# Spacers in three SBUF pools: the stationary and the moving operand of most 512-column products begin at the same place of 512 bytes

## Chip, cores and metric

The kernel runs on one core of a Trainium2 chip. The metric is the device time of one execution in microseconds, the median of the runs of a kernel. Three runs of the kernel before lie within 0.8 us of each other (1016.72 to 1017.52), so 0.2% (2.0 us) is about what a measurement of it can tell from no change.

## What is computed

One layer of an encoder block on 1024 tokens of width 1024, in float32:

```
h = rmsnorm(x) * (1 + sc1) + sh1;  u_f, q, k, v = split(h @ w_in)
y_f = per-group 2-D Fourier mix of u_f and a 64x64 map
y_a = windowed attention: softmax(q k^T / 8 + bias, sink) v, blocks of 128 queries against 384 keys
x   = x + g1 * (concat(y_f, y_a) @ w_out)
h2  = rmsnorm(x) * (1 + sc2) + sh2
16 experts, each picks its 128 best tokens:  y = (silu(xin @ w_gate) * (xin @ w_up)) @ w_down
x   = x + g2 * scatter_add(gate * y)
```

Each of the 48 expert matrices is 1024x1024 float32, 4 MB. They are read once each.

## The kernel before

**Products in three terms.** A float32 operand is split into a high part, which the matmul takes as fp32r, and a low part, the remainder. `mm3` (lines 73 to 76) multiplies a pair of split operands with three matmuls: high by high (line 74), low by high (line 75), high by low (line 76). The first argument after the output is the *stationary* operand (128 columns of activations, 512 bytes in each partition), the second the *moving* one (512 columns of weights, 2048 bytes in each partition). Each matmul loads its own stationary operand while the matmul ahead of it streams its moving one.

**Experts.** The weights come in units of 1 MB (256 rows of a matrix). `load` (line 1037) brings a unit into one of 13 `raw` buffers in three pools; `cut_unit` (line 1056) splits it: ScalarE writes `wh` (line 79), VectorE `wl` (line 80). The tile pair comes from the pool `wa` or from the pool `wk`, two buffers of each in either:

```
wp = wa if place[m] % 4 in (0, 1) else wk
h = wp.tile([128, 2, D], F32R, name="wh", bufs=2)
```

The first 6 units of all are used without a split (`PLAIN`, line 1214). `product` uses up one unit: 2 blocks of 128 rows, 2 halves of 512 columns, 3 matmuls each, 12 matmuls. A product of an expert is 4 units, 48 matmuls; an expert has three products (gate, up, down). By the line above the first two units of each product lie in `wk` and the last two in `wa`. The stationary operands of the experts, `t0h`, `t0l`, `t1h` and `t1l`, all lie in `wk`; experts take `t0` and `t1` in turns, and the down products take the one that is free. So each product is 24 matmuls with both operands in `wk`, then 24 with the stationary operand in `wk` and the moving one in `wa`. Split units: 186, of which 94 lie in `wa` and 92 in `wk`. TensorE, VectorE, ScalarE, GpSimd and the queue on SyncE each run their instructions in the order written.

**Attention and out-projection.** `front` (lines 677 and 678) makes the logits of a head: stationary `qk` from the pool `pb`, moving `khi` and `klo`, 384 or 256 columns. The out-projection `oproj` uses `mm3` with the stationary operands `yh`, `yl`, `yah`, `yal` (pool `p3`, which is on the right side of SBUF) and the moving `woh`, `wol` (pools `po0` and `po`, placed behind `pb`): 8 tiles of 128 tokens, 48 matmuls each. Its steps are put between those of the attention by a fixed rate.

**Input projection.** `terms` (line 367) multiplies, for one stationary tile `hh` or `hl`, three moving pieces of 512, 512 and 256 columns. Weights of blocks 0 to 3 lie in the pool `pw`, those of blocks 4 to 7 in `p1`, where `hh` and `hl` lie as well. The change doesn't touch it.

**Where the tiles begin.** Pools are filled from their start, tile by tile, so a tile's address in each partition follows from what stands before it. Its remainder by 512 bytes, as the built program has it (all steps inside these tiles are whole multiples of 512 bytes, but for the key blocks and head pieces, which don't matter here):

```
product               stationary   before   after    moving        before   after
experts, from wk      t0*, t1*       96      288     wh, wl (wk)      96      288
experts, from wa      t0*, t1*       96      288     wh, wl (wa)     288      288
out-projection        yh, yah ...     0        0     woh, wol        192        0
logits                qk             64      480     khi, klo        480      480
input projection 0-3  hh, hl        256      256     wh, wl          256      256
input projection 4-7  hh, hl        256      256     wh, wl           64       64
```

Of the kernel before, what the change touches and what calls it, by code (L numbers as in the profile page):

```python
# [11 lines left out]
F32 = mybir.dt.float32  # L12
# [33 lines left out]
def block_kernel(ctx: ExitStack, tc: tile.TileContext, t_in, out):  # L46
# [9 lines left out]
    def pool(name, bufs=1, space=None, **kw):  # L56
        if space is None:
            return tc.tile_pool(name=name, bufs=bufs, reuse_waits="tile", **kw)
        return tc.tile_pool(name=name, bufs=bufs, space=space, **kw)

    cst = ctx.enter_context(pool("cst"))
    dram = ctx.enter_context(pool("dram", space=bass.MemoryType.DRAM))
    ps = ctx.enter_context(pool("ps", bufs=2, space=bass.MemoryType.PSUM))
    raw1 = ctx.enter_context(pool("raw1", bufs=RAW1))

    def pt(name="pt"):
        return ps.tile([128, 512], F32, name=name, tag="pt", bufs=2)

    def banks(stack, name, **tags):
        p = stack.enter_context(pool(name, space=bass.MemoryType.PSUM))  # L70
        return [lambda t=t, n=n: p.tile([128, 512], F32, name=t, tag=t, bufs=n) for t, n in tags.items()]
# [62 lines left out]
    def drain(g):  # L134
        for _ in g:
            pass
# [202 lines left out]
    p = pt()  # L339
# [20 lines left out]
    def terms(ts, kc, hs_, o):  # L360
        for l, r in ((0, w_h), (1, w_h), (0, w_l)):
            for s_ in range(len(ts)):
                lhs = hs_[l][:, o + s_ * 128:o + s_ * 128 + 128]
                for acc, c0, c1 in zip(accs[s_], (0, 512, 1024), (512, 1024, 1280)):

                    first = kc == 0 and l == 0 and r is w_h and not (s_ and c0 == 1024)
                    PE.matmul(acc[:, :c1 - c0], lhs, r[kc][:, c0:c1], start=first, stop=(kc == 7 and r is w_l),  # L367
                              skip_group_check=c0 == 1024)
            yield
# [60 lines left out]
    p = terms(pair, 0, hs.pop(0), 0)  # L430
# [62 lines left out]
    for m, (t, kc0) in enumerate(seq):  # L493
# [20 lines left out]
        for a in range(4):  # L514
            project((t,), kc0 + a, hs_, a * 128)
            if m == 0 and a == 1:
                DVE.scalar_tensor_tensor(gg, qg, HD ** -0.5, kg, op0=OP.mult, op1=OP.mult)
                p = pt()
# [21 lines left out]
    pb = p_b.enter_context(pool("pb"))  # L540
# [6 lines left out]


    pj, lgb, ypb = banks(p_b, "psB", pj=2, lg=3, yp=1)

    st = {}

# [96 lines left out]
    def qprep(t, kv):  # L649
        pq = pt()  # L650
        for hp in range(2):
            PE.transpose(pq[:, hp * 128:hp * 128 + 128], qn[t][:, (kv * 2 + hp) * 128:(kv * 2 + hp + 1) * 128], ident)
        qk = pb.tile([128, 2, 2, 128], F32R, name="qk", bufs=2)
        pqv = pq[:, :256].rearrange("p (a b) -> p a b", b=128)
        for par in range(2):
            hi_r = slice(par * 64, par * 64 + 64)
            lo_r = slice(64 - par * 64, 128 - par * 64)
            ACT.activation(qk[hi_r, :, par, :], pqv[hi_r], AF.Copy)
            DVE.tensor_tensor(qk[lo_r, :, par, :], pqv[hi_r], qk[hi_r, :, par, :].bitcast(F32), op=OP.subtract)
        qks[t, kv] = qk  # L660

    def front(t, kv):
        blocks = span(t)
        k0 = blocks[0] * 128
        wid = len(blocks) * 128
        j0 = k0 - (t - 1) * 128
        qk = qks.pop((t, kv))
        m = pb.tile([128, 4], F32, name="m", bufs=4)
        negm = pb.tile([128, 4], F32, name="negm", bufs=4)
        den = pb.tile([128, 4], F32, name="den", bufs=4)  # L670
        es = pb.tile([128, 4], F32, name="es", bufs=4)
        rin = pb.tile([128, 4], F32, name="rin", bufs=4)
        sk = sink[:, kv * 4:kv * 4 + 4]
        sbs = []
        for i in range(4):
            lg = lgb()
            PE.matmul(lg[:, :wid], qk[:, i // 2, i % 2, :], khi[:, kv, k0:k0 + wid], start=True, stop=False)  # L677
            PE.matmul(lg[:, :wid], qk[:, i // 2, i % 2, :], klo[:, kv, k0:k0 + wid], start=False, stop=True)  # L678
            sb = pb.tile([128, 384], F32, name="sb", bufs=SB)
            DVE.tensor_tensor_reduce(sb[:, :wid], lg[:, :wid], bias[:, kv * 4 + i, j0:j0 + wid], 1.0,  # L680
                                     sk[:, i:i + 1], op0=OP.add, op1=OP.max, accum_out=m[:, i:i + 1])
            sbs.append(sb)
            tick()
        yield
        DVE.tensor_scalar(negm, m, -1.0, None, op0=OP.mult)
        DVE.tensor_tensor(es, sk, m, op=OP.subtract)
        ACT.activation(es, es, AF.Exp)
        for i in range(4):
            ACT.activation(sbs[i][:, :wid], sbs[i][:, :wid], AF.Exp, bias=negm[:, i:i + 1],
                           accum_out=den[:, i:i + 1])  # L690
        yield
        DVE.tensor_tensor(den, den, es, op=OP.add)
        DVE.reciprocal(rin, den)
        for i in range(4):
            DVE.tensor_scalar(sbs[i][:, :wid], sbs[i][:, :wid], rin[:, i:i + 1], None, op0=OP.mult)
        fr[t, kv] = sbs
# [43 lines left out]
    def load_x2(t):  # L740
        xh = raw([128, 2, D])
        SP.dma_start(xh[:, 0], x[t * 128:(t + 1) * 128, :])
        yt = at0.tile([128, 4, 128], F32, name="yt", tag="qn0")
        SP.dma_start(yt, ydf[t])
        yh = p3.tile([128, 4, 128], F32R, name="yh", bufs=2)
        yl = p3.tile([128, 4, 128], F32R, name="yl", bufs=2)
        split(yh, yl, yt)
        xts[t] = xh, yh, yl
# [178 lines left out]
    def wo_cut():  # L927
        k, j = divmod(next(wo_next), 2)
        split(wo_h[k][:, j], wo_l[k][:, j], wo_raw[k][:, j])
# [6 lines left out]
    def filler2():  # L936
        rate[0] = RATE2
        for t in range(NT):
            for i, _ in enumerate(oproj(t)):
                if t == 0 and i == 1:  # L940
                    g2_prep()
                if t == 0 and i == 5:
                    router_prep()
                for _ in range(2 if t > 4 else 1):
                    next(srt, None)
                yield
# [3 lines left out]
    def tick():  # L950
        debt[0] += rate[0]
        while debt[0] >= 1.0:
            debt[0] -= 1.0
            next(fill[0], None)
# [3 lines left out]
    srt = sorter()  # L958
    po, p3 = None, None
    po0 = p_c.enter_context(pool("po0"))  # L960
    wo_h, wo_l = ([po0.tile([128, 2, D], F32R, name=f"wo{x}{k}") for k in range(3)] for x in "hl")
    wo_next = itertools.count()
    wo_v = w_out.rearrange("(k p) c -> p k c", p=128)
# [13 lines left out]
    for n in range(len(units) + 2):  # L977
        if n == NSW:
            for _ in fill[0]:
                for g in lateq:  # L980
                    next(g, None)
            for g in lateq:
                drain(g)
            p_f.close()
            p_u.close()
            po = p_c.enter_context(pool("po"))
            p3 = p_c.enter_context(pool("p3", side="right"))
            sp[0] = p3
            g1_r, sh2_r, G2_r = (p3.tile([128, D], F32, name=n_) for n_ in ("g1_r", "sh2_r", "G2_r"))
            wr, wrG = (p3.tile([128, 8, NE], F32, name=n_) for n_ in ("wr", "wrG"))  # L990
            cb = p3.tile([128, NE], F32, name="cb")
            load_x2(0)
            for i, r in enumerate((g1_r, sh2_r, G2_r)):
                SP.dma_start(r, md[i:i + 1, :].to_broadcast([128, D]))
            wo_h.append(po.tile([128, 2, D], F32R, name="woh3"))
            wo_l.append(po.tile([128, 2, D], F32R, name="wol3"))
            wo_cut()
            wo_cut()
            fill = [filler2()]
            SP.dma_start(wr, t_in["w_router"][0].rearrange("(k p) e -> p k e", p=128))  # L1000
        fg = front(*units[n]) if n < len(units) else iter(())
        bg = back(*units[n - 2]) if n >= 2 else iter(())
        next(fg, None)
        next(bg, None)
        next(fg, None)
        next(bg, None)
        next(bg, None)
        drain(fg)
        for g in lateq:
            for _ in range(9):  # L1010
                next(g, None)
        if n + 1 < len(units):
            qprep(*units[n + 1])
            tick()
        drain(bg)
# [10 lines left out]
    wk = ctx.enter_context(pool("wk"))  # L1026
# [41 lines left out]
        load()  # L1068

    pa, = banks(ctx, "psM", pa=6)  # L1070
    for m in EARLY:
        load(m)
    g2_r = wk.tile([128, D], F32, name="g2_r")
# [218 lines left out]
    for b in range(2):  # L1292
        p = pt()
# [120 lines left out]
```

## Time and profile before

| what | value |
|---|---|
| median of three runs | 1017.39 us |
| the profiled execution's own time | 1017.5 us |
| its span, first to last instruction | 1015.4 us |
| TensorE busy | 958.8 us, 94% of the span |
| VectorE, ScalarE, GpSimd busy | 787.4, 628.0, 403.8 us |
| stages | the input projection's first product starts at 19.36 us, the last of the out-projection stage is over by 411.07, the first expert product starts at 428.11 |

The span is shorter than the time by 2.1 us, which lie around it. The busy time of a matmul in the profile has a modelled end and overlaps the next one; how fast matmuls follow one another is read from their starts, or from how many stand in a stretch in which TensorE never waits.

### The profile page before, as it was taken

How to read it: one execution, taken by the hardware profiler on the slowest of the kernel's cores; microseconds unless marked ns; L12 is line 12 of the kernel's file. 1: busy time of each engine (PE TensorE's matmuls, PEld its weight loads, DVE VectorE, ACT ScalarE, POOL GpSimd, SP SyncE). 2: the span in 40 equal slices, each digit the busy share in tenths (PEclk: the TensorE clock that was granted, in tenths of full speed). 3: DMA queues.
4: the chain of work that ended last, by engine and by line, in shares of the span. 5: the costliest groups of instructions: out<-in, count | busy, mean ns of one | idle time of the engine just before them, and what ended most of it. 6: DMA issues, size and time to landing. Idle time of an engine off the chain costs nothing.

```text
span 1015.4 us, 13138 instructions
## 1 busy us (share of the span) xinstructions
PE 958.8 (94%) x4737; PEld 747.6 (74%) x4737; DVE 787.4 (78%) x1240; ACT 628.0 (62%) x832; POOL 403.8 (40%) x236
## 2 busy tenths in 40 slices
PE   4997999979999999599899999999999999999996
PEld 3676877756777777458788888888888888888884
DVE  1346865777666869779869888988988898899894
ACT  2473444666455553226667777777777777777772
POOL 0026453100000000000357669768776876782203
PEclk9998999989999999599999999999999999999998
DMA  9966664361222138889989999999999999999912
GB/s 292 337 231 248 253 266 126 97 201 53 87 80 73 54 139 304 319 324 352 374 309 385 378 376 411 381 379 399 390 377 379 411 377 380 390 397 379 380 60 41
DMA packets 91641, 283.95 MB, mean 280 GB/s; under 512 B 8140, under 2 KB 25728, under 8 KB 91448
## 3 DMA queue, kind: packets, MB, share of 16 engines
q1 hardware_dynamic: 86712, 266.32, 69.3%
q0 software_dynamic: 4864, 16.80, 6.5%
q8 instruction: 37, 0.61, 0.2%
q14 instruction: 28, 0.23, 0.1%
HBM read 263.79 MB, written 21.40 MB: 281 GB/s over the span
## 4 chain that ended last, share of the span: by engine, by line
PE 83%; DVE 6%; POOL 3%; issue 2%; ACT 2%; DMA 1%; SPq 1%; POOLq 0%; ACTq 0%; DVEq 0%
PE pa L74 17%; PE pa L75 17%; PE pa L76 16%; PE pu L367 5%; PE pt L1258 3%; PE yp L719 3%; PE pj L75 2%; PE pj L74 2%; PE pa L1217 2%; PE pj L76 2%; PE pt L706 2%; PE pt L829 2%; PE lg L677 1%; DVE ws L116 1%; PE lg L678 1%
## 5 line engine op out<-in xcount | busy, mean ns | idle before, releaser
L80 DVE TENSOR_TENSOR wl<-raw,wh 128x2048 fp32r<-128x2048 f32 (+1 forms) x189 | 423.3, 2267 | 64.4 <-ACT wh L79 62.9
L79 ACT ACTIVATE wh<-raw 128x2048 fp32r<-128x2048 f32 (+1 forms) x189 | 355.7, 1895 | 79.0 <-PE pa L75 73.9
L1231 POOL TENSOR_SCALAR oneh<-tri_f,pos 128x128 bf16<-128x128 f32 x96 | 210.3, 2206 | 15.2 <-PE pt L1239 14.9
L74 PE MATMUL pa<-wh,t1h 128*128 128x512 f32 x384 | 152.5, 397 | 0.0
L76 PE MATMUL pa<-wl,t1h 128*128 128x512 f32 x384 | 150.7, 392 | 0.0
L75 PE MATMUL pa<-wh,t1l 128*128 128x512 f32 x384 | 150.6, 392 | 0.0
L74 PE MATMUL pa<-wh,t0h 128*128 128x512 f32 x360 | 144.8, 402 | 0.0
L75 PE MATMUL pa<-wh,t0l 128*128 128x512 f32 x360 | 142.3, 395 | 0.0
L76 PE MATMUL pa<-wl,t0h 128*128 128x512 f32 x360 | 142.2, 395 | 0.0
L792 POOL TENSOR_TENSOR rs<-ss,mhalf 128x1 f32<-128x1 f32 x8 | 4.4, 555 | 221.0 <-DVE ss L790 194.0
L1273 POOL TENSOR_TENSOR ys<-ys,g_r 128x512 f32<-128x512 f32 x30 | 53.5, 1800 | 91.6 <-ACT ys L1272 91.6
L76 PEld LDWEIGHTS pa<-wl,t1h 128*128 128x128 f32 x384 | 72.0, 188 | 16.5
L75 PEld LDWEIGHTS pa<-wh,t1l 128*128 128x128 f32 x384 | 72.1, 188 | 15.6
L74 PEld LDWEIGHTS pa<-wh,t1h 128*128 128x128 f32 x384 | 72.0, 188 | 15.6
L76 PEld LDWEIGHTS pa<-wl,t0h 128*128 128x128 f32 x360 | 68.2, 190 | 15.8
L75 PEld LDWEIGHTS pa<-wh,t0l 128*128 128x128 f32 x360 | 68.3, 190 | 14.9 <-issue 0.2
L74 PEld LDWEIGHTS pa<-wh,t0h 128*128 128x128 f32 x360 | 68.2, 189 | 14.9 <-issue 0.2
L1248 POOL DMA_INDIRECT xe<-h2d,idx x16 | 18.7, 1170 | 150.9 <-DVE gt L1245 150.8
L1276 POOL DMA_INDIRECT out_dram<-ys,idx x16 | 51.1, 3196 | 11.0 <-DVE ys L1275 6.6
L680 DVE CUSTOM_DVE_ANT_0 sb<-lg,bias,sink 128x384 f32<-128x384 f32 (+1 forms) x64 | 35.3, 579 | 16.9 <-PE pt L706 10.6
L367 PE MATMUL pu<-wh,hh 128*128 128x512 f32 x128 | 43.6, 422 | 2.3 <-ACT hh L79 2.1
L708 ACT ACTIVATE pT<-pt 128x512 f32<-128x512 f32 x44 | 25.5, 597 | 32.4 <-PE pt L706 32.2
(311 smaller groups left out, 1647.7 us busy)
## 6 DMA issues: line engine op xcount, KB each, us to landing
raw<-in_w_gate_dram SPq DMA_DIRECT2D x64, 1024.0 KB, 9.7
raw<-in_w_up_dram SPq DMA_DIRECT2D x64, 1024.0 KB, 8.1
raw<-in_w_down_dram SPq DMA_DIRECT2D x63, 1024.0 KB, 8.4
raw<-in_w_ada_dram SPq DMA_DIRECT2D x16, 1024.0 KB, 8.3
raw<-in_w_ada_dram SPq DMA_DIRECT2D x16, 512.0 KB, 8.9
xt<-in_x_dram SPq DMA_DIRECT2D x8, 512.0 KB, 5.0
raw<-in_w_out_dram SPq DMA_DIRECT2D x4, 1024.0 KB
raw<-in_x_dram SPq DMA_DIRECT2D x8, 512.0 KB
```

The source lines that it names most:

```text
L74: PE.matmul(o, lh, rh, start=start, stop=False)
L75: PE.matmul(o, ll, rh, start=False, stop=False)
L76: return PE.matmul(o, lh, rl, start=False, stop=stop)
L79: ACT.activation(hi, src, AF.Copy)
L80: return (eng or DVE).tensor_tensor(lo, src, hi.bitcast(F32), op=OP.subtract)
L367: PE.matmul(acc[:, :c1 - c0], lhs, r[kc][:, c0:c1], start=first, stop=(kc == 7 and r is w_l), skip_group_check=c0 == 1024)
L680: DVE.tensor_tensor_reduce(sb[:, :wid], lg[:, :wid], bias[:, kv * 4 + i, j0:j0 + wid], 1.0, sk[:, i:i + 1], op0=OP.add, op1=OP.max, accum_ ...
L719: PE.matmul(yp[par * 64:par * 64 + 64, :256], vf[:, b, kv * 64:kv * 64 + 64], pT[:, par * 256:par * 256 + 256], start=(bi == 0), stop=(bi ...
L1231: (POOL if t < shared else DVE).tensor_scalar(oneh[:, t, :], slots, pos[:, t, e:e + 1], None, op0=OP.is_equal)
L1258: PE.transpose(p[:, k * 128:k * 128 + 128], src[:, (4 * b + k) * 128:(4 * b + k + 1) * 128], ident)
L1273: POOL.tensor_tensor(ys[:, cs_], ys[:, cs_], g2_r[:, cs_], op=OP.mult)
L1276: POOL.indirect_dma_start(out=out2, out_offset=bass.IndirectOffsetOnAxis(ap=idx[:, :1], axis=0), in_=ys, in_offset=None, compute_op=OP.add)
```

## The change

Three small tiles that nothing reads or writes are set into pools, `spacer(p, n)` of n bytes in each partition: 416 in `pb` (behind `bias` and `sink`, ahead of everything else there), 416 in `po0` (ahead of the `wo` tiles), 192 in `wk` (ahead of all its tiles). A fourth call has 0 bytes and sets nothing. Since `po0` is placed behind `pb`, its tiles move by 832 bytes. The tiles of `wk` move by 192 bytes, those of `wa` and the `raw` pools don't move. The table above has the places.

```diff
+    spaced = itertools.count()
+
+    def spacer(p, n):
+        if n:
+            p.tile([128, n // 4], F32, name=f"spacer{next(spaced)}", bufs=1)
...
     pj, lgb, ypb = banks(p_b, "psB", pj=2, lg=3, yp=1)
+    spacer(pb, 416)
...
     po0 = p_c.enter_context(pool("po0"))
+    spacer(po0, 416)
...
             sp[0] = p3
+            spacer(p3, 0)
...
     pa, = banks(ctx, "psM", pa=6)
+    spacer(wk, 192)
     for m in EARLY:
```

The instructions of each engine are the same and stand in the same order. One wait is added. On ScalarE, at the first expert's SiLU (line 1330 before, 1341 after), `hs` now overlaps by 192 bytes what the last tile of the stage before left there. Before:

```order
 L79 ACTIVATE wh<-raw 128x2048 [waits DMAHW4_49]
 L1330 ACT_TABLE_LOAD [waits PE_49]
 L1330 ACTIVATE hs<-pa 128x512 [waits Pool_49]
 L1330 ACTIVATE hs<-pa 128x512 [waits PE_49]
 L79 ACTIVATE wh<-raw 128x2048 [waits DMAHW3_49,DVE_49]
```

After:

```order
 L86 ACTIVATE wh<-raw 128x2048 [waits DMAHW4_49]
 L1341 ACT_TABLE_LOAD [waits DVE_49,PE_49]
 L1341 ACTIVATE hs<-pa 128x512 [waits Pool_49]
 L1341 ACTIVATE hs<-pa 128x512 [waits PE_49]
 L86 ACTIVATE wh<-raw 128x2048 [waits DMAHW3_49,DVE_49]
```

No row has moved; the second one also waits for VectorE, for the normalisation at line 797 of the last token tile.

## Rows read from the trace of the kernel before

**Rows 1.** the page: busy us (share of the span) xinstructions of each engine

```profile
PE 958.8 (94%) x4737; PEld 747.6 (74%) x4737; DVE 787.4 (78%) x1240; ACT 628.0 (62%) x832; POOL 403.8 (40%) x236
```

**Rows 2.** waits of TensorE, experts' stage: who, for whom, total us, times, longest

```profile
PE pt L1239 <- DVE t1l L80: 3.5, 1, 3.5
```

**Rows 3.** stretches, one expert: us, busy PE, PEld, DVE, ACT, POOL, clock, DMA, GB/s

```profile
564.79:600.03 35.24, 35.24 (x169) 28.78 (x168) 31.14 (x23) 27.06 (x22) 26.60 (x13) 1.00 1.02 387
...
705.84:741.08 35.24, 35.24 (x170) 28.78 (x168) 31.16 (x23) 27.07 (x22) 26.59 (x13) 1.00 1.02 388
```

**Rows 4.** waits of TensorE in the attention stage (205 to 412 us), the longest

```profile
PE pt L818 <- DVE raw L783: 2.1, 1, 2.1
```

**Rows 5.** stretches of the attention stage, columns as in rows 3

```profile
225.00:300.00 75.00, 74.88 (x432) 55.27 (x429) 53.11 (x164) 44.58 (x124) 1.66 (x3) 1.00 0.22 76
300.00:410.00 110.00, 107.40 (x589) 80.22 (x587) 83.53 (x318) 53.32 (x141) 3.40 (x7) 0.96 0.41 151
```

**Rows 6.** timeline of TensorE at two boundaries in the experts: start, us, line, operation

```profile
700.38 0.39 PE L74 MATMUL pa<-wh,t1h 128*128 128x512 f32 x1
...
705.85 0.39 PE L74 MATMUL pa<-wh,t1h 128*128 128x512 f32 x1
```

**Rows 7.** stretches of 24 matmuls, experts: us, PE busy (x), clock, DMA, GB/s

```profile
694.78:700.38 5.60, 5.60 (x25) 1.00 1.03 411
700.38:705.84 5.46, 5.46 (x25) 1.00 1.02 410
...
730.02:735.62 5.60, 5.60 (x26) 1.00 1.02 410
```

**Rows 8.** the page's groups: matmuls of line 74 in the experts

```profile
L74 PE MATMUL pa<-wh,t1h 128*128 128x512 f32 x384 | 152.5, 397 | 0.0
...
L74 PE MATMUL pa<-wh,t0h 128*128 128x512 f32 x360 | 144.8, 402 | 0.0
```

**Rows 9.** chain that ended last, its final steps: start, us, what

```profile
993.63 0.70 ACT ys L1272
...
999.14 6.79 DMA out_dram<-ys,idx
```

**Rows 10.** a stretch of 36 out-projection matmuls, columns as in rows 7

```profile
382.14:390.54 8.40, 8.40 (x37) 1.00 0.82 330
```

**Rows 11.** groups by shape, attention stage: xcount | busy us, mean ns

```profile
L74 PE MATMUL pj<-woh,yah 128*128 128x512 f32 x48 | 21.5, 448 | 0.0
...
L677 PE MATMUL lg<-khi,qk 128*128 128x384 f32 x48 | 18.1, 377 | 0.1
```

**Rows 12.** the same chain: groups of eight transposes, start, us

```profile
454.00 0.87 PE pt L1258 x8
...
246.45 0.87 PE pt L706 x8
```

**Rows 13.** one line's instructions, ns min/median/max, 460 to 1000 us

```profile
L79 ACT ACTIVATE wh<-raw x181: 1046/1922/1941, 460.7 to 995.8; 128x2048 fp32r<-128x2048 f32 x179, 128x1024 fp32r<-128x1024 f32 x2
...
L80 DVE TENSOR_TENSOR wl<-raw,wh x182: 1769/2291/2437, 461.2 to 997.6; 128x2048 fp32r<-128x2048 f32 x180, 128x1024 fp32r<-128x1024 f32 x2
```

**Rows 14.** waits of ScalarE, VectorE and SyncE's queue, experts' stage (460 to 1016 us)

```profile
ACT wh L79 <- PE pa L75: 73.9, 75, 6.3
...
ACT wh L79 <- DMA raw<-in_w_down_dram: 1.7, 2, 0.8
...
DVE wl L80 <- ACT wh L79: 60.7, 75, 3.9
...
SPq L1053 <- DVE wl L80: 389.7, 155, 7.5
```

**Rows 15.** issue of unit loads (line 1053), 700 to 740 us, to landing

```profile
DMA to landing us min/median/max: 8.1/9.1/10.2
```

**Rows 16.** stretches of 36 input-projection matmuls, columns as in rows 7

```profile
131.83:138.84 7.01, 7.01 (x39) 1.00 0.23 80
156.25:163.25 7.00, 7.00 (x38) 1.00 0.00 0
```

## Prediction, made before the changed kernel ran

> **What bounds the kernel now.** I read the busy times first: TensorE is busy for 94% of the span, VectorE, the next, for 78% [rows 1]. Then the waits of TensorE, stage by stage. In the experts' stage, more than half of the span, it waits once, for 3.5 us [rows 2]; an expert takes 35.24 us of which TensorE is busy for all 35.24, at full clock, while VectorE has 31 and ScalarE 27 [rows 3]. In the attention stage its longest wait is 2.1 us [rows 4], and it is busy for 182.3 of 185 us [rows 5]. So in both stages the time is the number of matmuls times the distance from one start to the next, and only what changes this distance matters. The reader is to see next that the distance is not the same everywhere, though all these matmuls have one shape. A product of an expert has 24 matmuls whose operands both begin at 96 (weights in `wk`), then 24 with the stationary one at 96 and the moving one at 288 (weights in `wa`). The boundaries are found in the timeline by the stationary tile: it changes from t0h to t1h at 700.38, where a product begins, and is still t1h at 705.85, 24 matmuls later [rows 6]. From 694.78 to 700.38, the second half of a product, 24 matmuls take 5.60 us, 233 ns each; from 700.38 to 705.84, the first half of the next one, 5.46 us, 227.5 ns each; another second half again takes 5.60 [rows 7]. Clock and DMA share are the same in all of these. The distance differs by 5.8 ns, 70 ns a unit.
>
> **The change part by part.**
>
> *Experts.* After the change both operands begin at 288 in all split units. The counts of line 74 are 384 and 360 [rows 8], three times that is 2232 matmuls, 186 units; 94 of them are in `wa` and are 192 bytes apart now. If the distance follows from how far the two operands are apart, each of these gains 70 ns. Not all count. Eight of the 94 come before the one wait of TensorE [rows 2], which ends when a chain on VectorE ends; that chain starts from a product too, so I take half of them. Two belong to the last product of all, which isn't on the chain: it runs by way of `ys` of the product before it, from 993.63, and the scatter from 999.14 [rows 9]. That leaves 88 units times 0.070, **6.2 us**. An expert in steady state loses 6 times 0.070 and should take 34.82 us in place of 35.24.
>
> *Out-projection.* From 192 against 0 to 0 against 0. A stretch of 36 of these matmuls takes 8.40 us, 233 ns each [rows 10], the same as the pairs that are 192 apart in the experts, at other places. There are 48 of a kind [rows 11], eight kinds, 384. The gain lies between nothing (the input projection, below) and 384 times 5.8 ns, 2.2 us. Most of them stand in a row with others of their kind, but not all, and I take 4.5 ns each, **1.7 us**.
>
> *Logits.* From 64 against 480 to 480 against 480, 384 columns, 48 by 2 and some narrower ones, 112 in all [rows 11]. No row has such a pair at the same place. Bounds: nothing, and 112 times 5.8, 0.6 us. I take **0.2**, since each is followed by another operand or waits for VectorE.
>
> *What only moves.* The score tiles, `pT` and the tiles of `wk` begin elsewhere. Eight transposes take 0.87 us whether the tile begins at 96 (line 1258) or 192 (line 706) [rows 12]: nothing. ScalarE's and VectorE's cuts write to 288 and to 96 in turns, and their medians, 1922 and 2291 ns, are 1% and 6% from the maxima, 1941 and 2437 [rows 13], so the two places can't differ by more, on engines with room: nothing. The value product changes from 192 to 96 against 480 and 224 in turns; nothing in the trace prices that, and I allow 0.5 us either way.
>
> *The added wait.* ScalarE's first SiLU also waits for a normalisation on VectorE that ends before the experts begin; it already waits for a whole product. Nothing, and behind it on ScalarE stands only the next cut, which waits for TensorE anyway.
>
> *Who is late next.* A faster TensorE asks for 34.82 us an expert of VectorE's 31.2, and the cuts wait for TensorE (73.9 us of ScalarE, 60.7 of VectorE), not TensorE for them [rows 14]. The queue of loads waits 389.7 us for free buffers, ScalarE 1.7 us for loads [rows 14]; a load lands 8 to 10 us after its issue [rows 15] and its buffer comes round after 13 units, 13 times 35.24 / 12 or some 38 us. The transfers run at 387 GB/s on the mean of an expert [rows 3] and at 410 where products follow without a break [rows 7]; 387 times 35.24 / 34.82 is 392. So the gain should not be given back.
>
> *A rule against it.* The rows show that only the place of the weights differs between the two halves, and the time with it [rows 7]. The Trainium skill, "SBUF — State Buffer", section "Who interferes with whom", gives TensorE two read ports, one for the moving operand and one for the weight load, independent of each other, and says that it never waits on anyone. By it the place of the operands would cost nothing, and the change nothing either: 1017.5 us. The trace does not agree: 5.60 against 5.46 us.
>
> **The sum.** 6.2 + 1.7 + 0.2 = 8.1 us, from 1017.5 of the profiled execution: 1009.4. The median is 0.1 below that execution's time, so **1009.3 us**.
>
> **The rivals.**
>
> *Slower: the start of the moving operand itself sets the distance.* Rows so far: 96 is fast; 288 and 192 are slow. If 288 is slow as such, the wait for it now falls on all units: the 92 units of `wk` lose 0.070 each, 6.4 us, the out-projection stays at best: 1023.9. It decides as soon as the first half of a product takes 5.60. For it: in the experts the moving start and the distance between the operands change together, so the trace can't part them there. The input projection has both kinds too, at 256 against 256 and 64 against 256, and there 36 matmuls take 7.00 and 7.01 us [rows 16]. This speaks against any simple rule, and is why I don't go higher. But a third of those matmuls have 256 columns and leave half the time for the load of the next stationary operand, so a gain on the wide ones may be lost on the narrow ones. Against it: two pairs that are 192 apart, at different places, give the same 233 ns [rows 7, 10]. 9 in 100.
>
> *Half a gain.* Pairs at the same place differ among themselves, and 288 is less good than 96: if `wa` gains only 4 of the 5.8 ns and `wk` loses 1.7, two values that I choose between all and nothing, it is 88 times 0.048 less 92 times 0.020, 2.4 us, and with 1 us elsewhere 1014.1. The input projection speaks for it. 6 in 100.
>
> *Nothing, or another cause.* `wa` and `wk` are also different regions of memory, and the far one stays far: then the experts gain nothing and the time is 1017.4. Against it: in the out-projection and in blocks 0 to 3 of the input projection the operands lie in different pools as well, at 233 ns in the one and with no loss in the other. 5 in 100. The Trainium skill's rule above would end here too.
>
> *The transfers become the bound.* If 387 GB/s were all that can be had on the mean, some 5.6 of the experts' 6.2 us would be gone: 1014.9, and TensorE or the cuts would wait for loads. Against it are the 410 GB/s. 3 in 100.
>
> **How the numbers follow.** The forecast has the rest, 77 in 100. Its own range is 1007.5 to 1012, from the bounds above: 2.2 us in place of 1.7, 0.6 of 0.2, the eight early units whole, 0.5 of the value product on the good side; nothing in the attention stage and none of the early units on the other. To hold 8 in 10 the range takes in the half gain and the bound of the transfers too: 1007 to 1015 (half a microsecond below its own, for pairs after a slow half that the first halves now pay for). The bound of a measurable difference is 2.0 us, so up to 1015.4 is faster: forecast, half gain and transfers, 0.86 less a small part, 0.85; the same 0.06; slower 0.09.
>
> **What would show it.** Both halves of a product at 5.44 to 5.48 us, an expert at 34.8, 36 out-projection matmuls at 8.2, no new wait of TensorE, the line of the SiLU without a wait for VectorE. It is wrong if first halves go to 5.60 (the start itself), if second halves stay at 5.60 (region, or no cause at all), or if TensorE or ScalarE waits for loads.

## The result, and the profile after

The changed kernel takes 1008.38 us (median of 6 runs, 1005.25 to 1010.19) against 1016.89 us of the kernel before (6 runs, 1016.50 to 1017.52): the ratio is 0.9909, 95% interval 0.9894 to 0.9924. The forecast was 1009.3. The runs of after lie further apart than those of before; their mean granted clock goes from 0.969 in the slowest to 0.976 in the fastest. In every kernel below that ran more than once, but e1, the runs with a higher mean clock are on the whole the shorter ones. Beside the experiments the kernel before ran 46 more times, between 1014.20 and 1019.63 us: further apart than its first three. The profiled execution of after took 1009.72 us at 0.971, that of before 1017.5 us at 0.972.

Busy times on the page of after, which answer to [rows 1]:

```profile
PE 949.8 (94%) x4737; PEld 747.4 (74%) x4737; DVE 788.1 (78%) x1240; ACT 627.8 (62%) x832; POOL 404.7 (40%) x236
```

Only TensorE's busy time has moved by more than 1 us, by 9.0; the instructions are as many as before. Stretches of the experts in after: us, PE busy (x), granted clock, DMA share, GB/s. The first, second and last are halves of a product, the third is an expert.

```profile
691.38:696.82 5.44, 5.44 (x26) 1.00 1.02 410
696.82:702.26 5.44, 5.44 (x26) 1.00 1.02 410
702.26:737.00 34.74, 34.74 (x170) 1.00 1.03 394
726.12:731.56 5.44, 5.44 (x26) 1.00 1.02 410
```

Second halves went from 5.60 to 5.44 us. First halves, which had both operands at 96 already, went from 5.46 to 5.44 [rows 7]. An expert takes 34.74 us, 0.50 less than in [rows 3], and TensorE is still busy for all of it. The ends of the split products in the timelines of TensorE (start, us, line, operation), before:

```profile
450.64 0.80 PE L74 MATMUL pa<-wh,t0h 128*128 128x512 f32 x1
...
1004.44 0.39 PE L74 MATMUL pa<-wh,t1h 128*128 128x512 f32 x1
```

And after:

```profile
450.80 0.79 PE L81 MATMUL pa<-wh,t0h 128*128 128x512 f32 x1
...
996.52 0.39 PE L81 MATMUL pa<-wh,t1h 128*128 128x512 f32 x1
```

These are the first matmul of the first split unit and the third from the end of the last. Between them lie 553.80 us before and 545.72 after, 8.1 us less. Not all of it comes from the places. In both executions the granted clock fell to TensorE's lower level, 1.2 GHz, while TensorE stood in the one wait of the stage, and rose again to 2.4 GHz some microseconds behind it. The two stretches at the lower level, before and then after (us, PE busy (x), clock, DMA share, GB/s):

```profile
503.84:510.67 6.83, 6.31 (x22) 0.50 0.98 353
502.56:509.39 6.83, 5.34 (x20) 0.50 1.01 376
```

In after more of the stretch fell into the wait, and TensorE had 1.0 us less of work in it. Counted by the starts of matmuls, pair by pair, the pairs at the lower clock give 0.44 us of the 8.1, those at full clock 7.74, and the wait, longer by 0.09, takes that back: 7.7 us belong to the places. The waits in after, from 460 us on (TensorE from 440): who, for whom, total us, times, longest.

```profile
PE pt L1250 <- DVE t1l L87: 3.6, 1, 3.6
...
ACT wh L86 <- PE pa L82: 65.8, 70, 6.4
...
ACT wh L86 <- DMA raw<-in_w_gate_dram: 2.7, 3, 1.2
ACT wh L86 <- DMA raw<-in_w_down_dram: 1.6, 2, 0.8
...
ACT wh L86 <- DMA raw<-in_w_up_dram: 0.8, 1, 0.8
...
DVE wl L87 <- ACT wh L86: 52.8, 59, 3.9
...
SPq L1063 <- DVE wl L87: 384.4, 155, 7.4
```

TensorE has the one wait that it had [rows 2] and no new one. The reserve of the engines behind it has shrunk: ScalarE's wait for TensorE from 73.9 to 65.8 us, the loads' wait for free buffers from 389.7 to 384.4, and ScalarE now waits 5.1 us for loads in place of 1.7 [rows 14]. No wait of TensorE for it is in the trace.

Stages by TensorE, columns as in the stretches above: input projection, attention with the out-projection, and what lies between that and the first split unit. Before:

```profile
19.36:213.89 194.53, 179.42 (x920) 0.98 0.63 225
213.89:409.00 195.11, 191.65 (x1060) 0.96 0.35 125
409.00:450.64 41.64, 30.89 (x113) 0.72 0.80 301
```

After:

```profile
19.70:216.65 196.95, 181.99 (x921) 0.97 0.63 222
216.65:410.60 193.95, 189.76 (x1059) 0.97 0.35 126
410.60:450.80 40.20, 29.45 (x113) 0.75 0.82 308
```

The input projection, which the change doesn't touch, was 2.4 us longer in this execution, at a lower granted clock (0.97 against 0.98), and the two stages behind it 1.2 and 1.4 us shorter, at a higher one. A gain of a microsecond in these stages can't be read from one pair of executions; it has to be read from the starts of matmuls at full clock. Both kernels issue the same matmuls in the same order, so each distance from one start to the next can be set beside its counterpart; "at full clock" below counts those pairs for which neither execution was at the lower level.

### The profile page after: what moved, and what is told of

The parts are those of the page before. It is cut to its first block, busy times and chain, and to the rows that moved or that the text cites. A ratio compares the mean times of both kernels' runs of the same rounds, so it can differ in the third digit from the quotient of the medians.

```text
span 1007.6 us, 13138 instructions
## 1 busy us (share of the span) xinstructions
PE 949.8 (94%) x4737; PEld 747.4 (74%) x4737; DVE 788.1 (78%) x1240; ACT 627.8 (62%) x832; POOL 404.7 (40%) x236
## 4 chain that ended last, share of the span: by engine, by line
PE 83%; DVE 6%; POOL 3%; issue 2%; ACT 2%; DMA 1%; SPq 1%; POOLq 0%; ACTq 0%
PE pa L81 17%; PE pa L82 16%; PE pa L83 16%; PE pu L374 5%; PE yp L727 3%; PE pt L1269 3%; PE pj L81 2%; PE pj L82 2%; PE pt L714 2%; PE pj L83 2%; PE pa L1228 2%; PE pt L837 2%; PE lg L685 1%; DVE ws L123 1%; PE lg L686 1%
## 5 line engine op out<-in xcount | busy, mean ns | idle before, releaser
L86 ACT ACTIVATE wh<-raw 128x2048 fp32r<-128x2048 f32 (+1 forms) x189 | 355.4, 1896 | 73.7 <-PE pa L82 65.8
L1287 POOL DMA_INDIRECT out_dram<-ys,idx x16 | 50.8, 3174 | 10.9 <-DVE ys L1286 6.4
L278 ACT ACTIVATE hf<-pt,sh1c,G1c 128x128 f32<-128x128 f32 (+1 forms) x56 | 22.6, 480 | 38.7 <-PE pt L271 38.7
```

What stands on the lines that cost most here:

```text
L86: ACT.activation(hi, src, AF.Copy)
L1287: POOL.indirect_dma_start(out=out2, out_offset=bass.IndirectOffsetOnAxis(ap=idx[:, :1], axis=0), in_=ys, in_offset=None, compute_op=OP.add)
```

## Experiments

The theory: a 512-column matmul follows the one ahead at 227 ns where the stationary and the moving operand begin at the same place of 512 bytes, and at 233 elsewhere. The rivals: the start of the moving operand as such, the region of memory (`wa` against `wk`), the granted clock. Diffs are against the kernel before unless another is named; ratios are to it on the same chip.

### The spacer of wk alone, twice (e1_wk_only, e9_wk_again)

```diff
+    spacer(wk, 192)
     for m in EARLY:
```

> The spacer of 192 bytes in wk alone; both in the attention stage left out. Theory (the distance between the two operands' starts sets the interval): every split unit of the experts that no other work breaks takes 2.72 us as after the change, an expert 34.74, and nearly all of the gain is here: 8.1 us of the 8.5, 1008.8 from 1016.9. Rival (the prediction's own sizes, 6.2 us in the experts and 1.9 in the attention stage): 1010.7. Rival (the start of the moving operand itself): it would have shown already, since 288 is the start of all of them.

Measured: 1008.35 us (6 runs, 1007.85 to 1010.86) against 1016.98 (18 runs, 1014.25 to 1019.16), ratio 0.9921 (0.9903 to 0.9939). Two halves of a product in it, columns as above:

```profile
684.41:689.85 5.44, 5.44 (x25) 1.00 1.03 407
689.85:695.29 5.44, 5.44 (x25) 1.00 1.02 410
```

This spacer alone brings 8.6 us, as much as the whole change (8.5).

> The spacer in wk alone once more, beside the whole change on the same chip. Theory (the attention spacers shorten intervals by 0.8 us, the rest of their 4.7 us comes from falls of the granted clock that some executions have and others not): this lies 0.8 us above the whole change, with spreads that overlap; at the same mean clock the two differ by under 1 us. Rival (the 4.7 us are a gain of their own that adds): 4 to 5 us above it.

Measured: 1008.78 us (6 runs, 1005.32 to 1012.12) against 1017.53 (11 runs), ratio 0.9915 (0.9892 to 0.9938). At full clock the pairs of the experts' stage sum to 7.78 us less than before in e1 and in e9, to 7.74 to 7.77 less in the four traces of kernels with all spacers (after, e6, e7, e10), and to the same within 0.01 us in the traces of e2, e8 and e11, which have no spacer in `wk`.

### All pairs of the experts 192 apart (e3_all_apart)

`t0` and `t1` stay at 96, and the tiles of `wk` move to 288, where those of `wa` lie. So all pairs are 288 against 96.

```diff
     xh, xl = (wk.tile([128, 8, 128], F32R, name=f"t0{x}", bufs=1) for x in "hl")
+    spacer(wk, 192)
...
+        if e == 0:
+            spacer(wk, 320)
         hs = wk.tile([128, D], F32, name="hs", bufs=1)
```

> No spacer in the attention stage; in wk, spacers behind t0 (192) and ahead of hs and t1 (320), so that all moving operands of the experts begin at 288 and all stationary ones at 96: all pairs 192 bytes apart, with the moving operands where the change has them. Theory (distance): both halves of a product take 5.60 us, an expert about 35.7, and the time goes up by 92 units times 0.07, 6.4 us, to 1023.3. Rival (the start of the moving operand: 288 is good or bad as such): the same as after the change, 1008.8. Rival (the region of memory: weights of wk lie near the stationary tiles and those of wa far from them): as before, 5.46 and 5.60, 1016.9.

Measured: 1022.28 us (5 runs, 1020.73 to 1022.76), ratio 1.0050 (1.0031 to 1.0068). A first and a second half in it:

```profile
655.48:661.08 5.60, 5.60 (x26) 1.00 1.03 410
...
693.94:699.54 5.60, 5.60 (x26) 1.00 1.03 410
```

Both halves are slow, so it isn't the region: tiles of `wk` are slow too once they are 192 from `t0`. With after it settles the start as well: 288 is fast against 288 and slow against 96. In both kernels all split weights are written to 288 and read from there; of these products' operands only the stationary tiles begin elsewhere (96 and 288). So where the engines write the weights isn't the cause either. The time, 1022.28, is 1.0 below the expected 1023.3; at full clock the experts lost 6.2 of the expected 6.4 us.

### Other distances (e4_map1, e5_map2)

Three spacers in `wk` put `t0`, `t1` and the moving tiles of `wk` at 160, 480 and 416 (e4), and at 256, 384 and 352 (e5); those of `wa` stay at 288. Each kernel so has four distances, moving less stationary: 256, -64, 128, -192, and 96, -32, 32, -96. The edit of e4, that of e5 with 160, 96 and 32 in place of 64, 256 and 64:

```diff
+    spacer(wk, 64)
     xh, xl = (wk.tile([128, 8, 128], F32R, name=f"t0{x}", bufs=1) for x in "hl")
+    spacer(wk, 256)
...
+        if e == 0:
+            spacer(wk, 64)
         hs = wk.tile([128, D], F32, name="hs", bufs=1)
```

> No spacer in the attention stage; in wk, spacers of 64 ahead of t0, 256 behind it and 64 ahead of hs and t1, so that the moving operand begins 128 behind the stationary one for t0 with wa, 256 for t0 with wk, 64 ahead of it for t1 with wk and 192 ahead for t1 with wa. Theory (only the same place of 512 is fast): all four kinds of half take 5.60 us. Rival (the same place of 256): t0 with wk takes 5.44, the others 5.60. Rival (the same place of 128): t0 takes 5.44 with both, t1 5.60 with both. The time is between 1016 and 1024 by how many are fast.

> As the map before, with spacers of 160 ahead of t0, 96 behind it and 32 ahead of hs and t1: the moving operand begins 32 behind the stationary one for t0 with wa, 96 for t0 with wk, 32 ahead of it for t1 with wk, 96 ahead for t1 with wa. Theory, as the first map left it (the distance counts by its remainder by 256; 0 and 256 give 227 ns, a remainder of 64 gave 229, 128 and 192 gave 233): none of the four reaches 227, and a small distance, 32 or 224, is no better than a large one. Rival (what counts is that the two streams don't run close behind each other): the two of 32 are the slowest, over 233, the two of 96 lie at 229 to 233.

Measured, one run each: 1017.78 and 1021.81 us. Stretches of 12 matmuls in e4, at distances -64, -192, 256 and 128:

```profile
657.44:660.24 2.80, 2.80 (x14) 1.00 1.03 411
660.24:662.99 2.75, 2.75 (x13) 1.00 1.03 411
668.49:671.21 2.72, 2.72 (x14) 1.00 1.02 408
698.19:700.99 2.80, 2.80 (x13) 1.00 1.04 417
```

The same in e5, at -32, -96, 96 and 32:

```profile
658.06:660.86 2.80, 2.80 (x13) 1.00 1.02 410
660.86:663.66 2.80, 2.80 (x13) 1.00 1.03 411
669.27:672.07 2.80, 2.80 (x13) 1.00 1.03 413
699.33:702.13 2.80, 2.80 (x14) 1.00 1.02 410
```

So it is the distance, but by 256 and not by 512 bytes: 256 apart is as fast as the same place, 2.72 us for 12. The value -192, which is 64 by 256, lies between, at 2.75 (229 ns); the other six distances all take 2.80. The theory of e4, that only the same place of 512 is fast, was wrong, and its rival of 256 right but for -192; in e5 32 and 96 take the same, as its theory said, and the rival that the small ones are the slowest falls.

### The spacers of the attention stage without that of wk (e2_attention_only), and the out-projection alone (e8_out_projection_only)

Of the change, e2 keeps the spacers of `pb` and `po0`. e8 has only one, in `po0`:

```diff
     po0 = p_c.enter_context(pool("po0"))
+    spacer(po0, 320)
```

> The two spacers of 416 bytes alone, none in wk. The prediction's terms: out-projection 1.7 and logits 0.2 us, 1015.0 from 1016.9. Rival, from the trace after: the out-projection's matmuls come down to 227 ns only where many stand in a row without other matmuls between them, which is in the last three token tiles; 80 to 100 matmuls times 6 ns, 0.5 us, 1016.4, which can't be told from no change. Experts as before: halves of a product of 5.46 and 5.60 us.

> Of the change only the out-projection's part: one spacer of 320 bytes in po0, none in pb and wk, so that woh and wol begin at 0 and qk, the scores and pT where they were. Theory (direct gain only where many stand in a row): 36 in a row take 8.2 us in place of 8.4, the attention stage is shorter by 0.5 to 0.8 us, 1016.3. Rival (the 4.7 us of both spacers are real and come from the out-projection): 1012.3. Rival (they come from the logits, or from the scores and pT that move): 1016.9.

Measured: e2 1012.32 us (12 runs, 1010.47 to 1018.16), ratio 0.9961 (0.9944 to 0.9977); e8 1014.32 us (12 runs, 1010.17 to 1018.95), ratio 0.9976 (0.9959 to 0.9994). Neither time is what was expected (e2 1015.0 or 1016.4; e8 1016.3, or 1012.3 and 1016.9 by its rivals). e2 gains 4.7 us, more than twice what 5.8 ns on each of 384 matmuls would give, and with e1's 8.6 more than the whole change. So the sum of the parts doesn't fit, and the stage has to be looked at. A stretch of it, before:

```profile
321.00:333.00 12.00, 11.98 (x64) 0.87 0.34 132
```

The same in e2, and its whole stage:

```profile
321.00:333.00 12.00, 11.98 (x73) 1.00 0.33 130
...
213.43:404.31 190.88, 187.36 (x1060) 0.98 0.35 125
```

The kernel before got only part of TensorE's clock around 330, e2 all of it. In e8 the 36 matmuls that answer to [rows 10] take what its theory said, 8.2 us:

```profile
383.96:392.12 8.16, 8.16 (x38) 1.00 0.84 337
```

To tell the clock from the spacers, after and e1 were run again.

### After and e1 again (e6_after_again, e10_after_third, with e9 above)

> The changed kernel once more, beside the two that follow. If the gain of the two attention spacers alone (4.7 us measured, of which the trace shows some 0.8 us in shorter intervals and 3 us in two falls of the granted clock that came later or not at all) adds to that of wk alone (8.6), it is 1003.7. If the 3 us are chance of the clock, it stays near 1008.

> The changed kernel a third time, for the run beside it: 1008.4 by the two measurements so far; 1004 if the attention spacers' gain adds to that of wk.

Measured: e6 1008.80 us (6 runs, 1004.80 to 1011.08), ratio 0.9925 (0.9913 to 0.9938); e10 1007.61 us (6 runs, 1004.61 to 1011.08), ratio 0.9906 (0.9881 to 0.9931). The attention stage of the profiled executions of e6, of e10 and of e9, which has no spacer in this stage:

```profile
213.97:404.96 190.99, 187.47 (x1059) 0.98 0.35 125
```

```profile
214.15:405.32 191.17, 187.58 (x1059) 0.98 0.35 124
```

```profile
216.58:408.94 192.36, 188.29 (x1060) 0.98 0.34 121
```

At 0.98 the stage takes 191 us with the spacers and 192.4 without; at 0.96 to 0.97 it takes 194.0 with them (after) and 195.1 without (before). So most of the difference goes with the clock, which e9 got without the spacers, and two digits of it can't tell the rest. The pairs at full clock can: from the first to the last matmul of the out-projection they sum to 0.65 to 0.83 us less than before in the six traces with spacers in the stage (after, e2, e6, e7, e8, e10), and to the same within 0.02 us in e1, e3 and e9, which have none there. Of the 2.55 us by which this stretch is shorter in e2 than before, the pairs at the lower clock give 1.79. So the spacers of this stage bring some 0.7 us directly, and the rest of e2's 4.7 goes with the clock. Where e2 and the kernel before had the same mean clock over the execution, 0.973, e2 took 1014.4 and 1016.1 us (two runs) and before 1015.0 to 1016.5 (four runs on the same chip): less than 1 us apart. On one chip the whole change (e10) is 1.2 us ahead of the spacer of `wk` alone (e9), with intervals that overlap.

### The input projection as well (e7_inproj_too)

After with two more spacers, so that blocks 4 to 7 are 256 against 256 too. Against after:

```diff
     for k in range(8):
+        if k == 4:
+            spacer(p1, 192)
         w_h[k], w_l[k] = ((pw if k < 4 else p1).tile([128, 1280], F32R, name=f"w{x}{k}") for x in "hl")
+    spacer(p1, 320)
```

> The changed kernel with two more spacers in the pool p1 (192 ahead of the weights of blocks 4 to 7, 320 behind them), so that these too begin at 256, where hh and hl begin. Theory (a gain on products of 512 columns that the 256-column third gives back, since the load of the next stationary operand has half the time there): 36 matmuls of blocks 4 to 7 take 7.00 us in place of 7.01, and the time stays. Rival (the place counts for all alike): 36 times 5.8 ns, 0.2 us, less for each of 8 groups, 1.7 us in all.

Measured: 1006.97 us (6 runs, 1003.81 to 1008.90), ratio 0.9902 (0.9886 to 0.9919), the lowest median of all, but its interval overlaps that of e6 on the same chip, and its clocks reach 0.979. The 36 matmuls of blocks 4 to 7 that took 7.01 us in [rows 16] take 6.99:

```profile
132.20:139.19 6.99, 6.99 (x38) 1.00 0.25 91
```

So the direct gain is 0.02 us, as good as none. By the starts, three pieces of 512, 512 and 256 columns take 229, 233 and 124 ns at the same place, 586 in all, and 233, 236 and 118 ns apart, 587 in all: what the wide ones win the narrow one gives back. Why it does was not tried; the expectation's reason, the load of the next stationary operand, is not shown.

### The narrow piece made wide (e11_wide_third)

The third piece of the input projection is widened from 256 to 512 columns for tiles from 2 on; it repeats 256 columns of the second piece, which aren't used. Only stretches of it count, not its time (one run, 1025.13 us).

```diff
-                for acc, c0, c1 in zip(accs[s_], (0, 512, 1024), (512, 1024, 1280)):
+                for acc, c0, c1 in zip(accs[s_], (0, 512, 1024 if len(ts) > 1 else 768), (512, 1024, 1280)):
```

> No spacers. In the input projection of token tiles 2 to 7 the third piece is widened from 256 to 512 columns (768 to 1280; its first half only repeats a part of the second piece and is not used), so all three pieces are 512 wide; blocks 0 to 3 begin at the same place, blocks 4 to 7 192 apart. Theory (the narrow third gives the gain back): blocks 0 to 3 now take 227 to 229 ns a matmul and blocks 4 to 7 233, 36 of them 8.2 and 8.4 us. Rival (the input projection doesn't care for the place): both take the same. The time goes up by 144 matmuls of 256 more columns, some 15 us, and isn't compared.

24 matmuls of blocks 0 to 3 (256 against 256), then of blocks 4 to 7 (64 against 256):

```profile
150.15:155.59 5.44, 5.44 (x26) 1.00 0.00 0
78.78:84.27 5.49, 5.49 (x26) 1.00 1.05 369
```

With all pieces wide the two kinds do differ: 226.7 and 229 ns. The theory's 233 for blocks 4 to 7 was wrong, and e4 could have told it: 64 less 256 is -192, the distance that took 229 there. So the equal stretches of [rows 16] spoke against no rule of distance; the narrow piece hid it.

## Why the prediction was right, point by point

**What bounds.** Right. TensorE is busy for all of an expert in both kernels, so a shorter distance between matmuls came through whole, 0.50 us an expert.

**Experts, 6.2 us.** The mechanism is right, the term too small: 7.7. It counted 0.14 us a product (5.60 less 5.46) and took first halves as they were. Second halves gave 6.7 us, first halves 0.95, since 5.46 was a fast half that starts behind a slow one: in the kernel before the first five of these matmuls are 231 ns apart on the mean and the rest 227. So an expert gains 0.50 us, a product 0.17, and the 46.5 split products give 7.7. The prediction had this only as half a microsecond at the low end of its range. Nor had the early units to be halved: ahead of the one wait the starts gain 0.55 us, and the wait takes back 0.09 of it.

**Out-projection, 1.7 us.** The distance is right where the matmuls stand in a row. The 36 of after that answer to [rows 10], columns as above:

```profile
384.24:392.40 8.16, 8.16 (x37) 1.00 0.86 345
```

But 4.5 ns on each of 384 was too much. There are thirteen rows of nine or more without a break, 174 matmuls, and by the starts they are 0.56 us shorter in after, of which the longest row gives 0.24. The others stand between matmuls of the attention; with them it is 0.65 to 0.83 us, about 0.7. The step that failed is "most of them stand in a row with others of their kind": a row has to be long. In after seven of the thirteen never come to three distances of 226 to 228 on end, the others do behind one to ten; in the experts it is mostly three. The distances from start to start (ns) in one of the seven, before and after, and in the longest row after; the first column is the first start in us:

```
before  305.53   312 235 236 231 236 231 236 230
after   307.90   312 231 231 236 228 233 230 227
after   383.47   314 232 231 227 227 226 227 227 226 227 227 ...
```

**Logits, 0.2 us.** Nothing was found: the matmuls of `khi` and `klo` with 384 columns follow one another at 174 ns in both kernels.

**What only moves.** Right: the pairs of the stage that have to do with neither the out-projection nor the logits, the value product among them, sum to the same within 0.03 us at full clock in the six traces with spacers there.

**The added wait.** Right: nothing. What the first SiLU (its table load, to be exact) waited for by the profile, before and after:

```profile
ACT L1330 <- PE pa L1217: 11.9, 1, 11.9
...
ACT L1341 <- issue: 10.5, 1, 10.5
```

The second names no releaser, so the starts decide: the table load comes 9.7 us behind the start of the same 40 matmuls in both (443.56 behind 433.87, 443.71 behind 434.03), and the normalisation was over by 414, 30 us ahead.

**Who is late next.** Right: TensorE waits for no load at 394 GB/s over an expert, where the forecast had 392. The rival of the transfers falls; ScalarE's 5.1 us of waits for loads are where it would begin.

**The sum.** 7.7 and 0.7 are 8.4 us, and the medians differ by 8.5. That the forecast's 8.1 was so near is in part luck: 1.5 too little for the experts and 1.2 too much for the out-projection and the logits went against each other.

**The other rivals.** The start of the moving operand as such falls with after and e3, and so does the region, and half a gain. The Trainium skill's rule ("SBUF — State Buffer", section "Who interferes with whom": two independent read ports of TensorE, which never waits on anyone) as the prediction reads it, that the places cost nothing, does not hold for what these runs show: with the same instructions and transfers a half takes 5.44 or 5.60 us by the places of the two operands alone.

**What stays open.** Why the places matter was not tried; the runs show by which distance they do, not what in the chip makes it so. Nor is it settled whether the spacers in the attention stage make the higher clocks more frequent: four of e2's 12 runs, three of e8's and one of e7's six reach 0.978, none of the 46 runs of before on three chips exceeds 0.974, but e9 got 0.976 without them.

## What to carry to other kernels

Where TensorE is busy throughout and streams wide matmuls one after another, read their distance by the tiles that they use, and if one shape shows two distances, compare where stationary and moving tile begin: here equal places by 256 bytes took 227 ns in place of 233. Count such a gain only for long rows without a break and without a narrow matmul that gives it back, and count in the matmuls behind a slow stretch. A part of a change worth less than the spread of the granted clock is measured by the starts of its instructions, not by the median.

## What was not expected of the hardware

- As far as it was tried, the distance counts by 256 bytes: 0 and 256 apart give 2.72 us for 12 matmuls, -192 gives 2.75, and ±32, ±96, 128, -64 and 192 give 2.80.
- Fast pairs don't run fast at once: behind a break the starts are mostly 314, 232, 231 ns apart and then 227; in rows with pieces of 384 or 256 columns nothing is gained.
- Executions of one program differ by 6 us on one chip (e6: 1004.80 at a granted clock of 0.976, 1011.08 at 0.970). The three traces of this program show what goes with it: 1009.72, 1007.12 and 1004.80 us have 60.2, 52.8 and 50.8 us at the lower clock (1.2 GHz), and the same experts' stage within 0.02 us at full clock.
- The best distance that a row of 512-column matmuls settled at in any run was 226.7 ns. The Trainium skill ("TensorE: Matmul & The Clock Gate", section "Back-to-back issue gap") gives about 216 for an isolated 512-column matmul and about 131 for each in a stream; no row here, of fp32r matmuls that load a stationary operand each, comes to either.
